# A longer scan in the planner's table, and reciprocal norms spread by a repeated column

## The chip, the cores and the metric

The kernel runs on one core of a Trainium2 chip. The metric is the device time of one launch in microseconds; the kernel before took 1902.8 us, the median of three runs (1902.1 to 1905.98).

## The reference

Two layers of a backbone over 512 latent and 256 context tokens, 1024 channels, float32. Each layer: RMS norm with a modulation, one wide input projection, three mixers beside each other, a gated merge, an output projection and a residual add. A last RMS norm ends it.

```python
def rms_norm(x, g):
    y = xf * lax.rsqrt(jnp.mean(xf * xf, axis=-1, keepdims=True) + EPS)
    return (y * g).astype(x.dtype)

h = rms_norm(x, norm_g) * (1 + scale[:, None]) + shift[:, None]
aq, ..., gm = split_proj(h @ w_in)       # A: differential attention, B: mLSTM, C: neighbourhood attention
b = jnp.cumsum(lfc, axis=1)              # B: running sums of log forget gates, in chunks of 64
m_new = jnp.maximum(bL + m, jnp.max(g_s, axis=-1))   # B: and a running maximum over the chunks
x = x + gate[:, None] * merge_branches((y_a, y_b, y_c), gm, w_br, w_out)
```

The two parts that matter here are the norm, whose 1/rms is one number per token, and the mLSTM gates, whose running sums and maxima are scans over the 768 tokens.

## The kernel before

Activations are held transposed, channels on the partitions and tokens along the free axis, in eight tiles of 128 channels. A product in float32 is made of three matmuls of rounded halves (high by high, high by low, low by high); the low half of a weight tile (`wh<-wr,wh`) is subtracted on POOL or DVE, the high half cast on ACT. Each layer runs the branches C, A, B one after the other, then the merge, then the output projection ("finish"). In every branch the input projection of the next head (`pj<-h,wh`) is the filler of TensorE, and the attention of the heads before it (scores `gp<-qk` or `sc<-qk`, transposes `gp<-ident,p`, products with the values) is put between.

The order on each engine is written by a planner while the program is built. `Timed` (L324) wraps each engine and gives every instruction a price in ns (L341 to L349); `Sched` keeps one clock per engine, and lets a task issue its next TensorE instruction only when the planner's clocks say that its inputs are there. So a price that is too low makes the planner put dependent TensorE work too early; the engines run their lists in order, and on the chip TensorE then waits. The price of a VectorE instruction of n elements per partition is n / 0.96 + 69 ns; `tensor_tensor_scan` has no rule of its own. The lists are fixed at build time: nothing is reordered on the chip.

The three scans of a layer (L1409, L1411, L1418 in `branch_b_gates`) stand in the C branch on VectorE, between its softmax steps. The scores of C go through a ring of three PSUM tiles (`gp`): the fourth pair of scores can start only when ACT has taken the exponential of the first (`p<-gp,m`), and that waits for the row extremes (`m<-gp`) on VectorE. After the scans, twelve transposes `gp<-ident,pt` bring their results into columns, which VectorE copies to `bcol`.

`norm_rows` (L729) makes 1/rms: transposes of the summed squares, a reduction into columns (`ms`), nine small VectorE steps of `rsqrt_cols` that end in `rr` (128 tokens on the partitions, one column per block of tokens). To have it along the free axis on all partitions, it multiplies `ident` by each column into a diagonal matrix in a tile `dg` of the ring `p` (L746), and multiplies `ones` by it on TensorE (L751): row j of the result is r of token j everywhere. It is called once at the start (768 tokens, six blocks), twice at the end of layer 0 (512 and 256 tokens) and twice at the end of layer 1 (256 each).

Of the kernel before, what the change touches and what calls it, by code (L numbers as in the profile page):

```python
# [12 lines left out]
F32 = mybir.dt.float32  # L13
# [4 lines left out]
ALU = mybir.AluOpType  # L18
# [7 lines left out]
T = S + L  # L26
# [80 lines left out]
class Sched:  # L107
# [104 lines left out]
    def acq(self, tag, want=None, n=1):  # L212

        while True:
            now = self.T["P"] + (0.0 if want else self.EARLY)
            if not (want == "P" and self.late()) and sum(t <= now for t in self.free[tag]) >= n:
                break
            yield want
        for _ in range(n):
            self._take(tag, now)  # L220
# [5 lines left out]
    def wait(self, flag, n, want=None):  # L226
        while flag.n < n:
            yield want
        self.cur.t = max(self.cur.settle(), flag.t)
        yield want  # L230

    def hit(self, flag, n=1):
        flag.n += n
        flag.t = max(flag.t, self.stamp())
# [63 lines left out]
def _space(ap):  # L298
    return getattr(ap, "space", None)


def _elems(ap):
    n = 1
    for s in list(ap.shape)[1:]:
        n *= int(s)
    return n


class Timed:
# [5 lines left out]
    def __getattr__(self, name):  # L315
        f = getattr(self.real, name)

        def call(*args, **kw):
            aps = [v for v in list(args) + list(kw.values()) if hasattr(v, "shape")]
            n = max(_elems(v) for v in aps)  # L320
            small = sum(1 for v in aps if _elems(v) == 1 and n > 1)
            psum = any(_space(v) == PSUM for v in aps[1:] + aps[:1])
            writes = [kw["out"] if "out" in kw else args[0]]
            if "accum_out" in kw:  # L324
                writes.append(kw["accum_out"])
            if name == "tensor_tensor_reduce":
                writes.append(args[-1])
            reads = [v for v in aps if not any(v is w for w in writes)]
            if name == "dma_start":
                out = kw["out"]  # L330
                self.sched.dma(int(out.shape[0]), int(out.shape[0]) * _elems(out) * 4, reads, writes)
                return f(*args, **kw)  # L332
            if self.eng == "D":
                one = len([v for v in aps if _elems(v) == n]) <= 2 and name in ("tensor_copy", "tensor_scalar", "memset")
                cost = n / (1.92 if one and not psum else 0.96) + 69.0 + 61.0 * small
                if name == "reciprocal":
                    cost = 69.0 + 8.0 * n
                if name == "tensor_tensor_reduce":
                    cost += 220.0
            elif self.eng == "A":  # L340
                cost = n * 0.8333 + (51.0 if psum else 93.0) + 93.0 * small  # L341
            else:
                cost = n * 2.15 + 130.0
            self.sched.run(self.eng, cost, reads, writes)
            return f(*args, **kw)  # L345
        return call
# [3 lines left out]
def kernel(ctx: ExitStack, tc: tile.TileContext, a: dict, out: bass.AP):  # L350
# [10 lines left out]
    const = ctx.enter_context(tc.tile_pool(name="const", bufs=1))  # L361
# [4 lines left out]
    S_ = Sched(bufs)  # L366
    acq, rel, wait, hit = S_.acq, S_.rel, S_.wait, S_.hit
    V, ACT, GP, SY = (Timed(e, r, S_) for e, r in (("D", nc.vector), ("A", nc.scalar), ("G", nc.gpsimd), ("S", nc.sync)))

    def ring(tag, shape, dt=F32):  # L370
        t = rings[tag].tile([128] + list(shape), dt, tag=tag, name=tag)
        S_.fresh(tag, t)
        return t

    def small(n, name, dt=F32):
        return sm_.tile([128, n], dt, tag=name, name=name)

    def mm(o, l, r, start, stop, cost=None):
        n = _elems(o)
        S_.run("P", cost or (max(107.0, 0.4167 * n) + 2.0 if l.dtype != F32 else 1.67 * max(n, 128)), [l, r], [o])  # L380
        PE.matmul(o, l, r, start=start, stop=stop)  # L381

    def tr(o, i, idn):
        S_.run("P", 109.0, [i, idn], [o])
        PE.transpose(o, i, idn)  # L385
# [36 lines left out]

    ident = const.tile([128, 128], F32, name="ident")
    make_identity(nc, ident)
    ones = const.tile([128, 128], F32, name="ones")
    V.memset(ones, 1.0)

    V.memset(cfz, 0.0)
    cf = cfz[:, :, 0:2]
# [296 lines left out]
            rel("t")  # L726
        hit(aflag)

    def norm_rows(acc, n, dg, aflag, res, nflag, tags):  # L729

        nt = n // 128
        yield from wait(aflag, KD, "P")
        ms, r = small(NT, "ms"), small(NT, "rr")
        for t0 in range(0, nt, 4):
            m = min(4, nt - t0)
            yield from acq("gp", "P")
            p = ring("gp", [512])
            for b in range(m):
                tr(p[:, 128 * b:128 * b + 128], acc[:, 128 * (t0 + b):128 * (t0 + b) + 128], ident)
            yield  # L740
            V.tensor_reduce(ms[:, t0:t0 + m], p[:, :128 * m].rearrange("p (b d) -> p b d", d=128), axis=AX.X, op=ALU.add)
            rel("gp")
        V.tensor_scalar(ms[:, :nt], ms[:, :nt], 1.0 / D, EPS, ALU.mult, ALU.add)
        yield from rsqrt_cols(r[:, :nt], ms[:, :nt], nt, "rt")
        for b in range(nt):
            V.tensor_scalar(dg[:, 128 * b:128 * b + 128], ident, r[:, b:b + 1], None, ALU.mult)  # L746
        for o in range(0, n, 512):
            w = min(512, n - o)
            yield from acq("gp", "P")
            p = ring("gp", [512])  # L750
            mm(p[:, :w], ones, dg[:, o:o + w], True, True)  # L751
            res.append(p[:, :w])
        hit(nflag)
        for t in tags:
            rel(t)
# [35 lines left out]
    def layer(l, x, h, hfl):  # L791
# [942 lines left out]
        def finish(mh, mhf):  # L1734
            S_.need("qk"), S_.need("qk")
            xs, pairs = x_tiles()
            for k in range(KD):
                SY.dma_start(out=xs[k][:, :nq], in_=xin[:, k, :nq] if l == 0 else xdr[k])
            S_.need("p"), S_.need("p")
            acc, dg = ring("p", [T]), ring("p", [T])  # L1740
            fs = [[Flag(), Flag()] for _ in range(KD)]
            for s, (o, n) in enumerate(wsegs(l)):
                kind = 0 if o < S else 1
                aflag, nflag, res = Flag(), Flag(), []
                for d in range(KD):
                    def done(si, ps, o, n, d=d, kind=kind, aflag=aflag):
                        def fin():
                            xd = xs[d][:, o:o + n]
                            yield from wait(modf[l][4 + d // 4], 1)
                            V.scalar_tensor_tensor(xd, ps[:, :n], modc[l][:, 16 + d, kind:kind + 1], xd, ALU.mult, ALU.add)  # L1750
                            rel("pj")
                            yield "S"
                            if not last and kind == 0:
                                SY.dma_start(out=xdr[d], in_=xd)
                                S_.cur.landed = 0.0
                            yield from sumsq(acc[:, o:o + n], xd, aflag, d)
                        S_.urgent(fin())
                    proj(("wout", d, s), [(o, n)], done, mh, ready=lambda k: need(mhf[k][kind]))
                S_.calm(norm_rows(acc[:, o:o + n], n, dg[:, o:o + n], aflag, res, nflag, ("p", "p") if s else ()))
                row = lambda res=res: res[0]  # L1760
                if not last:
                    all_h(l + 1, s, xs, mh, row, nflag, fs)
                    continue

                def give(k, o=o, n=n, row=row, nflag=nflag):
                    yield from wait(nflag, 1)
                    for i in range(k, k + 2):
                        xd = xs[i][:, o:o + n]
                        V.scalar_tensor_tensor(xd, xd, prm[0][:, PRM_FG + i:PRM_FG + i + 1], row(), ALU.mult, ALU.mult)
                        yield None if i == k else "S"  # L1770
                    SY.dma_start(out=out[:, k:k + 2, o:o + n], in_=pairs[k // 2][:, :, o:o + n])
                for k in range(0, KD, 2):
                    S_.calm(give(k))
            return xs, mh, fs
# [4 lines left out]
        return finish(*merge())  # L1779


    S_.need("p"), S_.need("p")
    acc, dg = ring("p", [T]), ring("p", [T])
    aflag, nflag, res = Flag(), Flag(), []
    for k in range(KD):
        S_.calm(sumsq(acc, x0[k], aflag, k))
    S_.calm(norm_rows(acc, T, dg, aflag, res, nflag, ("p", "p")))
    h, hfl = [], [[Flag(), Flag()] for _ in range(KD)]
    for k in range(KD):
        S_.need("h")  # L1790
# [124 lines left out]
```

## Time and profile before

| | |
|---|---|
| median of the runs | 1902.8 us |
| the profiled execution | 1903.77 us, span 1902.0 us |
| TensorE busy | 1813.3 us, 95% of the span |
| VectorE busy | 1343.8 us, 71% |
| ScalarE, GpSimd busy | 858.0 us, 643.1 us |
| mean granted TensorE clock | 0.987 |

The profile describes one execution. PE is TensorE's matmuls, PEld its weight loads, DVE VectorE, ACT ScalarE, POOL GpSimd. Nearly all lines read L345 (the wrapper's call), L381 (matmul) or L385 (transpose), since helpers issue everything; what an instruction does is read from the tiles' names and shapes. In a timeline, a row merges neighbours of a kind (x is their count), and the bracket at its end says how long the engine stood idle before it and which engine's instruction ended that. Scans are shown by the order listing as SCALAR_TENSOR_TENSOR and by the trace as TENSOR_TENSOR_SCAN.

### The profile page before, as it was taken

What the parts mean: (1) busy time and instruction counts of PE and PEld (TensorE: products, weight loads), DVE (VectorE), ACT (ScalarE), POOL (GpSimd) and SP (SyncE); (2) the same over time, 40 slices, a digit from 0 to 9 for tenths busy, and PEclk for the clock granted to TensorE, in tenths of its full rate; (3) what the DMA queues carried; (4) which work ended last, traced back from release to release, by engine and by line L of the source; (5) the groups of instructions that cost most, each with busy time, mean ns of one, the idle gap of its engine ahead of it and who ended that gap; (6) DMA issues with size and microseconds to landing.
All of it is one profiled execution on the core that took longest, in us unless ns stands there. A gap on an engine that the chain in (4) does not pass through costs nothing. (4 is left out here: it accounts for less than half of the span.)

```text
span 1902.0 us, 31909 instructions
## 1 busy us (share of the span) xinstructions
PE 1813.3 (95%) x11140; PEld 1602.3 (84%) x11140; DVE 1343.8 (71%) x3168; ACT 858.0 (45%) x1932; POOL 643.1 (34%) x563
## 2 busy tenths in 40 slices
PE   5999999999999999999999889999999899999996
PEld 2989998988899888888888778898888787888886
DVE  6676767888887875777763887766887788733346
ACT  4455555555555453222233354644555444533343
POOL 1332322221223322333335343423212324344454
PEclk9999999999999999999999899999999999999998
DMA  8333422222342443666546334333222434545453
GB/s 324 91 106 97 116 81 82 64 78 65 104 118 82 118 154 126 220 195 202 193 153 217 112 98 124 108 92 101 76 67 62 145 89 131 158 159 162 160 169 127
DMA packets 148479, 243.56 MB, mean 128 GB/s; under 512 B 18400, under 2 KB 52544, under 8 KB 148320
## 3 DMA queue, kind: packets, MB, share of 16 engines
q1 hardware_dynamic: 148320, 241.53, 40.8%
q8 instruction: 88, 1.44, 0.3%
q14 instruction: 71, 0.58, 0.1%
HBM read 199.45 MB, written 27.33 MB: 119 GB/s over the span
## 5 line engine op out<-in xcount | busy, mean ns | idle before, releaser
L381 PE MATMUL pj<-h,wh 128*128 128x512 f32 (+1 forms) x5664 | 1110.6, 349 | 3.1 <-ACT h L345 1.8
L381 PEld LDWEIGHTS pj<-h,wh 128*128 128x128 f32 x5664 | 895.7, 191 | 122.0 <-ACT h L345 2.4
L345 POOL TENSOR_TENSOR wh<-wr,wh 128x512 fp32r<-128x512 f32 (+1 forms) x409 | 562.3, 1382 | 1114.4 <-ACT wh L345 1066.6
L345 ACT CAST wh<-wr 128x512 fp32r<-128x512 f32 (+1 forms) x416 | 256.4, 621 | 377.9 <-PE pj L381 213.1
L381 PE MATMUL pj<-wh,h 128*128 128x256 f32 (+1 forms) x1728 | 239.4, 290 | 6.3 <-DVE h L345 4.9
L381 PEld LDWEIGHTS pj<-wh,h 128*128 128x128 f32 x1728 | 220.8, 193 | 10.1 <-DVE h L345 7.3
L345 DVE TENSOR_TENSOR pt<-gp,pt 128x512 fp32r<-128x512 f32 (+1 forms) x224 | 123.9, 572 | 87.4 <-ACT pt L345 86.4
L345 ACT CAST pt<-gp 128x512 fp32r<-128x512 f32 (+1 forms) x224 | 105.5, 496 | 151.7 <-PE gp L385 151.1
L381 PE MATMUL pj<-v,wh 128*128 128x512 f32 (+1 forms) x576 | 159.7, 356 | 0.1
L385 PE MATMUL gp<-ident,p 128*128 128x128 f32 x720 | 110.6, 276 | 17.6 <-DVE p L345 11.8
L381 PE MATMUL gp<-pt,v 128*128 128x256 f32 x864 | 117.4, 283 | 0.1
L381 PEld LDWEIGHTS pj<-v,wh 128*128 128x128 f32 x576 | 102.9, 189 | 15.6 <-DVE t L345 0.5
L385 PEld LDWEIGHTS gp<-ident,p 128*128 128x128 f32 x720 | 84.3, 141 | 36.1 <-issue 17.5
L381 PEld LDWEIGHTS gp<-pt,v 128*128 128x128 f32 x864 | 110.8, 191 | 2.3 <-DVE pt L345 0.3
L345 ACT ACTIVATE t<-pj 128x512 f32<-128x512 f32 (+1 forms) x118 | 63.5, 538 | 102.1 <-PE pj L381 100.7
L381 PE MATMUL pj<-qk,wh 128*128 128x512 f32 (+1 forms) x288 | 102.4, 356 | 0.8 <-DVE qk L345 0.7
L345 DVE SCALAR_TENSOR_TENSOR t<-t,pj 128x512 f32<-128x512 f32 x66 | 38.5, 594 | 75.4 <-PE pj L381 75.4
L381 PE MATMUL sc<-qk 128*128 128x512 f32 (+1 forms) x360 | 83.3, 340 | 7.8 <-ACT p L345 4.9
L345 DVE TENSOR_REDUCE mna<-sc 128x1 f32<-128x768 f32 (+1 forms) x80 | 67.7, 846 | 31.1 <-PE sc L381 30.7
L345 ACT ACTIVATE p<-sc,mna 128x768 f32<-128x768 f32 (+1 forms) x80 | 65.6, 820 | 47.4 <-DVE mna L345 47.1
L345 DVE CUSTOM_DVE_ANT_0 sc<-cb,dt 128x512 f32<-128x512 f32 x56 | 58.9, 1052 | 33.0 <-DMA cb<-in_wmodr_dram 31.8
L345 DVE CUSTOM_DVE_ANT_0 sc<-cb,prm 128x512 f32<-128x512 f32 x56 | 61.5, 1099 | 26.1 <-DMA cb<-in_wmodr_dram 24.8
(145 smaller groups left out, 2095.0 us busy)
## 6 DMA issues: line engine op xcount, KB each, us to landing
wr<-in_wu_dram SPq DMA_DIRECT2D x296, 256.0 KB, 2.9
cb<-in_wmodr_dram SPq DMA_DIRECT2D x64, 256.0 KB, 3.7
wr<-in_wout_dram SPq DMA_DIRECT2D x64, 256.0 KB, 2.9
p<-afd SPq DMA_DIRECT2D x80, 192.0 KB, 4.2
wr<-in_wbr_dram SPq DMA_DIRECT2D x48, 256.0 KB, 2.8
q<-qk SPq DMA_DIRECT2D x160, 64.0 KB, 2.2
cb<-vd SPq DMA_DIRECT2D x32, 256.0 KB, 3.3
qk<-in_xT_dram SPq DMA_DIRECT2D x16, 384.0 KB, 6.3
```

Source lines behind the costliest of these rows:

```text
L345: return f(*args, **kw)
L381: PE.matmul(o, l, r, start=start, stop=stop)
L385: PE.transpose(o, i, idn)
```

## The change

A scan of n elements is now priced at n / 0.48 + 430 ns, which for 768 elements is 2030 ns in place of 869 ns. And `norm_rows` no longer makes the diagonal: the column `rr` is repeated 128 times (a stride of zero) as the stationary operand and `ident` is the moving one, one matmul of 128 columns for each block. The tiles `dg` and `ones` go. Both change what the planner's clocks say, so the order changes downstream as well.

```diff
@@ Timed.call
                 if name == "tensor_tensor_reduce":
                     cost += 220.0
+                if name == "tensor_tensor_scan":
+                    cost = n / 0.48 + 430.0
...
-    ones = const.tile([128, 128], F32, name="ones")
-    V.memset(ones, 1.0)
...
-    def norm_rows(acc, n, dg, aflag, res, nflag, tags):
+    def norm_rows(acc, n, aflag, res, nflag, tags):
...
         yield from rsqrt_cols(r[:, :nt], ms[:, :nt], nt, "rt")
-        for b in range(nt):
-            V.tensor_scalar(dg[:, 128 * b:128 * b + 128], ident, r[:, b:b + 1], None, ALU.mult)
         for o in range(0, n, 512):
             w = min(512, n - o)
             yield from acq("gp", "P")
             p = ring("gp", [512])
-            mm(p[:, :w], ones, dg[:, o:o + w], True, True)
+            for b in range(o // 128, (o + w) // 128):
+                mm(p[:, 128 * b - o:128 * b - o + 128], r[:, b:b + 1].to_broadcast([128, 128]), ident, True, True)
             res.append(p[:, :w])
...
@@ finish, and the start likewise
-            S_.need("p"), S_.need("p")
-            acc, dg = ring("p", [T]), ring("p", [T])
+            S_.need("p")
+            acc = ring("p", [T])
```

In the listings the line numbers shift: L345, L381 and L385 of before are L347, L383 and L387 now.

First place: TensorE in the C branch of layer 0, from the third to the fourth pair of scores of the branch (`gp<-qk` and `gp<-qk,q`, two matmuls each), with projection work between. Before:

```order
L381 MATMUL gp<-qk,q_858 128x256 x2
L381 MATMUL pj<-h,wh 128x512 x3
L381 MATMUL pj<-h,wh 128x256 x6
L381 MATMUL gp<-qk 128x256 x2
L381 MATMUL gp<-qk,q_858 128x256 x2
L381 MATMUL pj<-h,wh 128x256 x18
```

And now:

```order
L383 MATMUL gp<-qk,q_852 128x256 x2
L383 MATMUL pj<-h,wh 128x512 x3
L383 MATMUL pj<-h,wh 128x256 x18
L383 MATMUL gp<-qk 128x256 x2
L383 MATMUL gp<-qk,q_852 128x256 x2
L383 MATMUL pj<-h,wh 128x256 x6
```

Twelve projection matmuls of 256 columns have moved ahead of the fourth pair.

Second place: the same pairs of scores on TensorE in the C branch of layer 1. Before:

```order
L381 MATMUL gp<-qk,q_12732 128x256 x2
L381 MATMUL pj<-h,wh 128x256 x6
L381 MATMUL pj<-h,wh 128x512 x3
L381 MATMUL gp<-qk 128x256 x2
L381 MATMUL gp<-qk,q_12732 128x256 x2
L381 MATMUL pj<-h,wh 128x512 x18
L385 MATMUL gp<-ident,pt 128x112 x2
```

And now:

```order
L383 MATMUL gp<-qk,q_12724 128x256 x2
L383 MATMUL pj<-h,wh 128x256 x6
L383 MATMUL pj<-h,wh 128x512 x21
L383 MATMUL gp<-qk 128x256 x2
L383 MATMUL gp<-qk,q_12724 128x256 x2
L383 MATMUL pj<-h,wh 128x512 x6
```

Eighteen projection matmuls of 512 columns have moved ahead of the fourth pair, and the transposes `gp<-ident,pt` stand 33 projection matmuls behind that pair in place of 18.

The same place on VectorE, from the third scan (`v<-v,pt 112x768`) to the row extremes `m` that release the fourth pair. Before:

```order
L345 SCALAR_TENSOR_TENSOR v<-v,pt 112x768
L345 TENSOR_TENSOR v<-pt,v 112x768
L345 COPY pt<-v 48x768
L345 TENSOR_REDUCE m_12802<-gp 128x1
L345 ISA p,m_12805<-gp,cb,m_12802 128x256
```

And now:

```order
L347 SCALAR_TENSOR_TENSOR v<-v,pt 112x768
L347 TENSOR_REDUCE m_12792<-gp 128x1
L347 ISA p,m_12795<-gp,cb,m_12792 128x256
L347 ISA m_12795 128x1
L347 TENSOR_REDUCE m_12809<-gp 128x1
L347 ISA p,m_12812<-gp,cb,m_12809 128x256
L347 TENSOR_TENSOR v<-pt,v 112x768
```

The extremes now stand right behind the scan, ahead of the add and the copy. In layer 0 the same two rows have moved behind them.

Third place: TensorE at the end of layer 0, from the transposes of the first norm to its spread (`gp<-p,ones` before, `gp<-ident,rr` now). Before:

```order
L385 MATMUL gp<-ident,p 128x128 x4
L381 MATMUL pj<-h,wh 128x256 x54
L381 MATMUL gp<-p,ones 128x512
L381 MATMUL pj<-h,wh 128x256 x102
L381 MATMUL pj<-wh,h 128x272 x36
```

And now:

```order
L387 MATMUL gp<-ident,p 128x128 x4
L383 MATMUL pj<-h,wh 128x256 x42
L383 MATMUL gp<-ident,rr 128x128 x4
L383 MATMUL pj<-h,wh 128x256 x114
L383 MATMUL pj<-wh,h 128x272 x36
```

The spread stands twelve projection matmuls earlier. The other three norms' spreads stand: at the start one matmul earlier, ahead of the columns of the modulation (`gp<-csel,t`); in the second norm of layer 0 where they stood; in the first norm of layer 1 six matmuls earlier; at the very end where it stood.

In layer 0 the order of attention work against projection work differs in branch C and early in branch A, and is the same again from there to the layer's end; in layer 1 it differs from the scans to the end of branch B. Of the low halves of the weights, two move from VectorE to POOL (six and 402 of 128x512 before, four and 404 now).

## Rows read from the trace of the kernel before

**Rows 1.** Page: span, and busy time by engine

```profile
span 1902.0 us, 31909 instructions
...
PE 1813.3 (95%) x11140; PEld 1602.3 (84%) x11140; DVE 1343.8 (71%) x3168; ACT 858.0 (45%) x1932; POOL 643.1 (34%) x563
```

**Rows 2.** Timeline of PE: start, us, what, [idle before <-releaser]

```profile
100.15 0.80 PE L381 MATMUL gp<-qk 128*128 128x256 f32 x2 [3.02 <-ACT p L345]
...
1042.39 6.71 PE L381 MATMUL pj<-h,wh 128*128 128x256 f32 x54
...
1052.25 2.08 PE L381 MATMUL gp<-p,ones 128*128 128x512 f32 x2 [3.15 <-DVE p L345]
...
1105.31 16.62 PE L381 MATMUL pj<-h,wh 128*128 128x512 f32 x72
...
1134.27 0.80 PE L381 MATMUL gp<-qk 128*128 128x256 f32 x2 [6.94 <-ACT p L345]
...
1893.81 1.19 PE L381 MATMUL gp<-p,ones 128*128 128x256 f32 x2 [3.50 <-DVE p L345]
```

**Rows 3.** Waits of PE: who for whom, us in total, times, longest

```profile
PE gp L381 <- ACT p L345: 10.7, 3, 6.9
...
PE gp L385 <- DVE bcol L345: 1.9, 2, 1.3
```

**Rows 4.** Windows: stretch, length, busy PE PEld DVE ACT POOL, then PEclk, DMA, GB/s

```profile
100.00:104.00 4.00, 3.85 (x21) 3.85 (x22) 3.61 (x14) 2.84 (x9) 0.57 (x1) 0.61 0.31 74
...
1052.20:1056.00 3.80, 3.75 (x14) 2.71 (x15) 2.45 (x5) 0.77 (x2) 0.00 (x0) 0.58 0.24 86
...
1134.00:1138.00 4.00, 3.73 (x12) 3.20 (x13) 3.75 (x12) 3.16 (x8) 1.28 (x1) 0.58 0.47 130
```

**Rows 5.** Windows in layer 1, branches A and B

```profile
1370.00:1390.00 20.00, 16.71 (x78) 13.29 (x77) 15.91 (x38) 8.28 (x20) 2.95 (x2) 0.83 0.19 53
1390.00:1662.00 272.00, 258.85 (x1547) 224.55 (x1545) 218.96 (x549) 137.81 (x310) 86.66 (x86) 1.00 0.39 113
```

**Rows 6.** Lines of DVE: group xcount | busy, mean ns | idle before

```profile
L345 DVE TENSOR_TENSOR_SCAN pt<-pt,t 112x768 f32<-112x768 f32 x4 | 7.5, 1904 | 0.1
...
L345 DVE TENSOR_SCALAR p<-ident,rr 128x128 f32<-128x128 f32 x16 | 5.5, 401 | 0.1
```

**Rows 7.** Timeline of ACT: the exponential behind the layer-1 extremes

```profile
1133.66 0.47 ACT L345 ACTIVATE p<-gp,m 128x256 f32<-128x256 f32 x1 [8.23 <-DVE m L345]
```

**Rows 8.** Timeline of DVE around the third scan, layer 0 then layer 1

```profile
96.26 1.23 DVE L345 TENSOR_TENSOR v<-pt,v 112x768 f32<-112x768 f32 x1
97.50 0.90 DVE L345 COPY pt<-v 48x768 f32<-48x768 f32 x1
98.43 0.42 DVE L345 TENSOR_REDUCE m<-gp 128x1 f32<-128x256 f32 x1
...
1127.20 1.91 DVE L345 TENSOR_TENSOR v<-v,pt 112x767 f32<-112x767 f32 x1
1129.15 1.82 DVE L345 TENSOR_TENSOR_SCAN v<-v,pt 112x768 f32<-112x768 f32 x1
1131.00 0.96 DVE L345 TENSOR_TENSOR v<-pt,v 112x768 f32<-112x768 f32 x1
1131.97 0.56 DVE L345 COPY pt<-v 48x768 f32<-48x768 f32 x1
1132.56 0.42 DVE L345 TENSOR_REDUCE m<-gp 128x1 f32<-128x256 f32 x1
```

**Rows 9.** Timeline of DVE at the diagonals: end of layer 0, end of layer 1

```profile
1049.40 2.79 DVE L345 TENSOR_SCALAR p<-ident,rr 128x128 f32<-128x128 f32 x4
...
1893.18 0.48 DVE L345 TENSOR_SCALAR p<-ident,rr 128x128 f32<-128x128 f32 x2
```

**Rows 10.** Timeline of PEld at the last spread

```profile
1893.78 0.50 PEld L381 LDWEIGHTS gp<-p,ones 128*128 128x128 f32 x2 [3.71 <-issue]
```

**Rows 11.** Timeline of POOL beside the scans of layer 1

```profile
1126.31 1.98 POOL L345 TENSOR_TENSOR wh<-wr,wh 128x512 fp32r<-128x512 f32 x1
```

More of the change, by code (lines that the diff above doesn't have):

```diff
@@ L1758, in finish @@
                     proj(("wout", d, s), [(o, n)], done, mh, ready=lambda k: need(mhf[k][kind]))
-                S_.calm(norm_rows(acc[:, o:o + n], n, dg[:, o:o + n], aflag, res, nflag, ("p", "p") if s else ()))
+                S_.calm(norm_rows(acc[:, o:o + n], n, aflag, res, nflag, ("p",) if s else ()))
                 row = lambda res=res: res[0]
@@ L1779, in layer @@
         return finish(*merge())
-    S_.need("p"), S_.need("p")
-    acc, dg = ring("p", [T]), ring("p", [T])
+    S_.need("p")
+    acc = ring("p", [T])
     aflag, nflag, res = Flag(), Flag(), []
@@ L1786 @@
         S_.calm(sumsq(acc, x0[k], aflag, k))
-    S_.calm(norm_rows(acc, T, dg, aflag, res, nflag, ("p", "p")))
+    S_.calm(norm_rows(acc, T, aflag, res, nflag, ("p",)))
     h, hfl = [], [[Flag(), Flag()] for _ in range(KD)]
```

## The prediction

> **What bounds the kernel now.** I read the page first, then TensorE's waits, then its timeline for the idle pieces, then windows behind the long ones, and last VectorE and POOL at those places. TensorE is busy for 1813.3 of 1902.0 us [rows 1], so the span is its work plus 88.7 us in which it stands. The matmul work is nearly the same after the change, so I ask only which of those idle microseconds go, and which come. The reader is to see that the waits are few and long in three places: at the fourth pair of scores in branch C, once in each layer (3.02 and 6.94 us), and at the first spread at the end of layer 0 (3.15 us); 3.50 us at the last spread lies on the way to the end [rows 2]. The two score waits are nearly all of a single row among the waits, PE for ACT's exponential; the columns of the scan results cost 1.9 us more [rows 3].
>
> A long wait costs twice. Behind each of the three the granted clock is 0.61, 0.58 and 0.58 of full speed over about 4 us, a mix of the 1.2 and the 2.4 GHz level [rows 4], so work that would go at full speed loses 4.0 x 0.39 = 1.6, 3.8 x 0.42 = 1.6 and 4.0 x 0.42 = 1.7 us. Waits short enough leave the clock: from 1390 to 1662 us TensorE stands for 272 - 258.9 = 13.1 us in all, and the clock reads 1.00 [rows 5].
>
> **Part one: the price of the scan.** The chip takes 1.9 us for a scan [rows 6], the planner charged 0.87 us and now charges 2.03 us. No scan gets faster; what pays is that TensorE's list stops asking for results the chip does not have. Why TensorE stood: ACT's exponential waited 8.23 us for the row extremes [rows 7], which stood behind the scans on VectorE, and there behind an add and a copy that nobody on TensorE needs soon [rows 8].
>
> Layer 0. The fourth pair is reached 12 matmuls of 256 columns later; one takes 6.71 / 54 = 0.124 us [rows 2], so 1.5 us. The extremes no longer wait for the add and the copy, 1.23 + 0.90 = 2.1 us [rows 8]. Together 3.6 us against a wait of 3.02 us: it goes, and with it the slow clock. 3.0 + 1.6 = 4.6 us.
>
> Layer 1. The pair is reached 18 matmuls of 512 columns later, 18 x 16.62 / 72 = 4.2 us [rows 2], and the extremes come 1132.56 - 1131.00 = 1.6 us earlier [rows 8]. Left of 6.94 us: 1.2 us, too little to pull the clock, by the short waits of [rows 5]. Gain 5.8 + 1.7 = 7.5 us. The wait for the columns (1.9 us) goes as well, since the transposes now have 33 projection matmuls ahead of them behind that pair, not 18: 9.4 us for layer 1. The lower bound here is that only the moved order counts and the clock falls again: 4.2 us.
>
> The work passed over is not lost: the projection matmuls that move ahead are TensorE's own, done in the time it stood. On VectorE the add and the copies come later, and what waits for them are the columns, whose transposes are later too. Two weight halves move to POOL, on an engine that is busy for 643 of 1902 us [rows 1]; I cost them at nothing, and at 4.0 us if TensorE should come to wait for both, at the 1.98 us of one [rows 11].
>
> **Part two: the spread.** Sixteen VectorE instructions of 0.401 us go [rows 6], 6.4 us of an engine that is off the path at most times. What counts is where each norm ends.
>
> End of layer 0. The reciprocals were ready when the four diagonals began, at 1049.40; the diagonals ended 2.79 us later [rows 9], and the spread began at 1052.25 after 3.15 us of idle time [rows 2], so TensorE arrived at 1049.1. Now it arrives 12 x 0.124 = 1.5 us earlier, at 1047.6, and starts at about 1049.5, with those 1.5 us of work still to do: 1052.25 - 1049.5 - 1.5 = 1.3 us gained. It stands for 1.9 us rather than 3.15, so I take the clock as kept: 1.3 + 1.6 = 2.9 us, with 1.3 us if it falls. VectorE, which makes the next layer's `h` behind it, starts 2.8 us earlier too, so I see nothing that takes this back.
>
> The last norm. Two diagonals, 0.48 us [rows 9], go from the path to the end. Against it: two weight loads become four, at 0.25 us each [rows 10], hidden or not; 0 to 0.5 us, I take 0.3. The start, the second norm of layer 0 and the first of layer 1: the spread is ready earlier by the diagonals that stood before it, and TensorE has about as much more work behind it as it waits less. I take 0; at the start the bounds are the six diagonals, 6 x 0.401 = 2.4 us of gain, and a loss of 1.0 us for eight more weight loads at 0.25 us of which half show.
>
> The loads are where the Trainium skill speaks against the change: "TensorE: Matmul & The Clock Gate", section Weight-path perf modes, says that the fast weight load is not used for float32. By that rule all the new loads stay slow, as the float32 loads of `ones` were; the trace agrees in that those took 0.25 us each [rows 10]. If none were hidden the last norm would give 0.0 in place of 0.3.
>
> **The sum.** 4.6 + 9.4 + 2.9 + 0.3 = 17.2 us. Against it stands what the new order costs in the stretches it shuffles: I take 3 us, one wait as long as that of layer 0's scores, because work that TensorE now reaches sooner is made by engines that did not get faster. 17.2 - 3 = 14.2 us off 1903.8 us (the profiled execution) is 1889.6; that execution is 1.0 us above the median of the runs, 1902.8, which becomes 1888.6. I say 1889 us.
>
> **The rivals.** *The layer-1 stall stays in part.* For: VectorE is late there for a reason that the planner still has no price for. The subtraction ahead of the third scan took 1.91 us where the add of that shape behind it took 0.96 us [rows 8], and POOL's weight half lay beside it from 1126.31 to 1128.29 [rows 11]. If three such instructions stretch by about 0.95 us each, the extremes come 2.9 us later, the wait left is 4.1 us and the clock falls again: 2.9 + 1.7 = 4.6 us less, 1894 us. The Trainium skill has a rule for it, in "SBUF — State Buffer", section SBUF: two separate sides: VectorE and GpSimd share a port pair under an exclusive lock, and the loser waits for the winner's whole instruction. The trace agrees in that one row pair; by the rule the stretch depends on where POOL's work falls, which shifts with the order. Against: the 18 matmuls alone cover 4.2 us.
>
> *It is given back.* TensorE reaches the branches A and B of layer 1 some 9 us ahead of where it was, while VectorE is busy there for 219 of 272 us [rows 5]. If the 13.1 us of idle time there become 28 us, about 2 us of the 17.2 remain: 1901 us. For: that stretch has the densest waits left. Against: an engine at 80% can catch up, and the planner again places work where its clocks allow.
>
> *Slower.* The shuffle makes new stalls with a fall of the clock in branches A and B. One cluster of that kind stands there now, from 1370 to 1390 us: 3.3 us idle and a clock of 0.83, together 3.3 + 20 x 0.17 = 6.7 us [rows 5]. Three more of these cost 20.1 us and outweigh 17.2; with four the time is 1903 + 26.8 - 17.2 = 1912 us. It decides from the third. For: the order differs from the scans of layer 1 to the end of its branch B. Against: 2.5 of them would be needed merely to break even, and there is one in the whole of layer 1's attention.
>
> **How the numbers follow.** Forecast 0.57, the stall in part 0.14, given back 0.16, slower 0.11, and 0.02 for a shuffle that also removes the cluster at 1370. Runs of this kernel tell about 0.2%, 3.8 us, from no change. Faster: 0.57 + 0.14 + 0.02 = 0.73; the same 0.16; slower 0.11. The low end is the full sum with one lucky 6.7 us cluster gone, 1902.8 - 17.2 - 6.7 = 1879; the high end takes in most of the second rival, 1902. That leaves out less than 2 in 10.
>
> **What would show it.** Right: TensorE's waits for ACT's exponential at `gp<-qk` fall from 10.7 us to under 2 us, the clock reads 1.00 behind the scans of both layers, the columns' wait is gone, the first spread of layer 0 waits for `rr` under 2 us, TensorE's busy time falls by some 5 us (less slow clock) and its idle time by 8 to 12 us. Wrong: the windows behind the fourth pair still read 0.6; or they read 1.00, and the idle time from the scans of layer 1 to the end of its branch B has grown by more than 10 us.

## The result, and the profile after

The changed kernel takes 1893.8 us, the median of five runs (1891.98 to 1895.11), beside 1902.8 us for the kernel before on the same chip (1900.84 to 1905.98): a ratio of 0.9946, 95% interval 0.9932 to 0.996. It is faster by 9 us, about 0.5%. The forecast was 1889 us, 1879 to 1902 in range. The profiled execution took 1891.98 us.

The page of the changed kernel, to be read against [rows 1]: TensorE's busy time fell by 3.9 us, and what it stood fell from 88.7 to 1890.2 - 1809.4 = 80.8 us.

```profile
span 1890.2 us, 31916 instructions
...
PE 1809.4 (96%) x11160; PEld 1606.1 (85%) x11160; DVE 1324.6 (70%) x3149; ACT 859.5 (45%) x1932; POOL 647.1 (34%) x565
```

TensorE's waits in it (who for whom, us in total, times, longest), to be read against [rows 3]:

```profile
PE gp L387 <- DVE p L347: 12.0, 16, 2.2
PE gp L383 <- DVE rr L347: 8.7, 4, 3.0
PE gp L387 <- DVE pt L347: 8.6, 2, 6.7
...
PE gp L383 <- ACT p L347: 3.8, 3, 1.6
```

The wait for ACT's exponential fell from 10.7 to 3.8 us; the forecast was under 2. And a row that was not among the long ones, the transposes' wait for VectorE's `pt`, now has 8.6 us. TensorE's timeline shows where, and answers to [rows 2]: the first row stands at layer 0's fourth pair of scores (3.02 us before), the second at the transposes of the scan results behind it, the third at the spread that ends layer 0 (3.15 before), then layer 1's third and fourth pairs (6.94 before at the fourth), the new wait, and the last spread (3.50 before).

```profile
109.45 0.50 PE L383 MATMUL gp<-qk 128*128 128x256 f32 x2 [0.84 <-ACT p L347]
...
118.17 0.60 PE L387 MATMUL gp<-ident,pt 112*128 112x112 f32 x4 [1.94 <-DVE pt L347]
...
1045.97 1.16 PE L383 MATMUL gp<-ident,rr 128*128 128x128 f32 x8 [1.76 <-DVE rr L347]
...
1126.40 0.50 PE L383 MATMUL gp<-qk 128*128 128x256 f32 x2 [1.42 <-ACT p L347]
...
1131.25 0.51 PE L383 MATMUL gp<-qk 128*128 128x256 f32 x2 [1.56 <-ACT p L347]
...
1131.82 4.27 PE L383 MATMUL pj<-h,wh 128*128 128x512 f32 x18
1135.94 0.60 PE L387 MATMUL gp<-ident,p 128*128 128x128 f32 x4
1143.19 1.11 PE L387 MATMUL gp<-ident,p 128*128 128x128 f32 x4 [6.65 <-DVE pt L347]
...
1881.99 1.20 PE L383 MATMUL gp<-ident,rr 128*128 128x128 f32 x4 [2.98 <-DVE rr L347]
```

So layer 1's stall did not go: it ends 12 us behind the start of the fourth pair, at the transposes of the softmax rows and no longer at the scores, and nearly kept its length. The windows that answer to [rows 4] say the same of the clock: 1.00 behind the fourth pair of layer 0 and at the norm (0.61 and 0.58 before), 0.76 around the new wait. In the branches behind, the clock reads 1.00 from 1370 to 1390 us (0.83 in [rows 5]), and over the 272 us behind that TensorE stands for 7.8 us, not 13.1.

```profile
105.00:125.00 20.00, 16.93 (x105) 14.20 (x103) 18.76 (x54) 10.04 (x25) 5.40 (x6) 1.00 0.40 114
1045.00:1060.00 15.00, 14.03 (x117) 14.03 (x118) 12.92 (x20) 10.12 (x20) 10.75 (x8) 1.00 0.49 143
1138.00:1152.00 14.00, 8.81 (x60) 8.81 (x61) 10.84 (x38) 3.06 (x10) 1.81 (x3) 0.76 0.23 72
1370.00:1390.00 20.00, 18.54 (x112) 15.96 (x111) 18.72 (x42) 10.23 (x25) 5.01 (x4) 1.00 0.32 87
1390.00:1662.00 272.00, 264.21 (x1566) 229.63 (x1564) 219.10 (x580) 141.44 (x319) 88.08 (x89) 0.99 0.39 115
```

The cluster of stalls that stood at 1370 us is not simply gone, though. One of its kind stands some 30 us earlier in the changed kernel, and before has none there; TensorE's timeline and the window behind it:

```profile
1338.92 0.85 PE L387 MATMUL gp<-ident,p 128*128 128x128 f32 x6 [2.25 <-DVE p L347]
1341.39 0.72 PE L383 MATMUL sc<-qk 128*128 128x512 f32 x2 [1.62 <-ACT p L347]
```

```profile
1340.00:1350.00 10.00, 8.61 (x34) 7.07 (x35) 6.48 (x20) 3.32 (x8) 0.00 (x0) 0.83 0.01 2
```

What VectorE does from the second scan to the `pt` that ends the wait (its timeline in the changed kernel, cut to the rows that matter; in the whole list no gap of over 0.2 us stands between two rows):

```profile
1117.41 2.03 DVE L347 TENSOR_TENSOR_SCAN pt<-pt,t 112x768 f32<-112x768 f32 x1
1119.47 1.22 DVE L347 TENSOR_TENSOR v<-pt 112x768 f32<-112x768 f32 x1
1120.73 1.94 DVE L347 TENSOR_TENSOR v<-v,pt 112x767 f32<-112x767 f32 x1
1122.70 2.09 DVE L347 TENSOR_TENSOR_SCAN v<-v,pt 112x768 f32<-112x768 f32 x1
1124.71 0.39 DVE L347 TENSOR_REDUCE m<-gp 128x1 f32<-128x256 f32 x1
...
1126.63 1.89 DVE L347 TENSOR_TENSOR v<-pt,v 112x768 f32<-112x768 f32 x1
...
1131.60 0.56 DVE L347 COPY pt<-v 48x768 f32<-48x768 f32 x1
...
1134.85 1.96 DVE L347 COPY pt<-v 48x768 f32<-48x768 f32 x2
...
1137.56 1.25 DVE L347 TENSOR_SCALAR p<-p,smc 128x512 f32<-128x512 f32 x1
...
1141.37 1.16 DVE L347 COPY pt<-v 64x512 f32<-64x512 f32 x4
1142.46 0.68 DVE L347 TENSOR_TENSOR pt<-gp,pt 128x512 fp32r<-128x512 f32 x1
```

From 1117.41 to 1142.46 us are 25.05 us of VectorE; the planner's clock gave the same rows 20.9 us. TensorE's list was built for a VectorE 4.1 us further on.

Since the order differs, equal times in two kernels are not equal work. The ledger below gives each matmul the time that its form usually takes from one start to the next (the 40th percentile over all runs; the spreads' own matmuls count as nothing), and compares the moments at which TensorE has done the same sum. Entries are microseconds gained (-) or lost (+) against before in that stretch, whose ends are times of before: C of layer 0 is 80 to 135, the rest of layer 0 to 1030, its last norm to 1100, C of layer 1 to 1160, the rest to 1840. A row adds up to the difference of the two profiled spans. They come from one execution each; two with one list differ by up to 3 at the start and about 2 in another stretch. The profiled run of before is 1.0 us above its median, that of the changed kernel 1.8 us below, so the first row adds up to 11.8 us where the medians give 9.0; that of the planner with POOL's overlap is 5.5 us above, that of the price alone 2.6 us.

| kernel | start | C, layer 0 | rest | norm | C, layer 1 | rest | end |
|---|---|---|---|---|---|---|---|
| changed | +2.1 | -0.3 | -5.2 | -2.9 | +0.2 | -5.7 | 0.0 |
| price alone | +3.0 | -0.2 | -5.3 | +0.3 | +0.8 | -3.8 | +0.4 |
| spread alone | +1.5 | +0.2 | -2.0 | -1.6 | +1.4 | -0.4 | -0.7 |
| VectorE charged 4.1 us | +1.5 | -4.4 | +7.8 | -1.5 | +0.7 | -2.5 | -0.2 |
| planner with POOL's overlap | +3.9 | -0.5 | +10.3 | +1.4 | +6.0 | -9.9 | -2.2 |
| price 2250 | +1.3 | -2.3 | +3.1 | -2.8 | -0.3 | -1.0 | -0.3 |
| price in layer 1 only | +0.8 | +1.1 | -2.0 | -2.6 | +0.4 | -4.9 | -0.3 |
| changed, copies on ACT | +0.6 | -2.7 | -4.9 | -2.6 | -3.2 | -4.7 | -0.3 |
| changed, POOL empty there | +1.1 | +0.7 | -5.6 | -1.6 | -7.2 | -3.7 | -0.5 |
| before, copies on ACT | 0.0 | -0.9 | -1.6 | -1.3 | -3.6 | -0.3 | +0.5 |
| copies on ACT, new plan | +2.8 | -2.6 | +7.9 | -2.9 | -5.6 | -12.0 | -0.7 |

The first row tells the result: the two C branches, where the price was meant to act, are worth nothing, the norm's entry is what was forecast, and the rest comes from branches that have no scan in them. Two entries say less than they seem to. Of the 5.2 us in the rest of layer 0 about 2 belong to the one execution of before: the three runs with its order there (the spread alone, the price in layer 1 only, before with copies on ACT) have 1.6 to 2.0 as well. And at the norm a kernel that keeps the diagonals (before with copies on ACT) has 1.3. In layer 1, by the same reckoning in finer steps, the cluster at 1370 us gives about 5 us and the new one at 1338 us takes about 5; what is left of the gain arises behind 1420 us.

### The profile page after: what moved, and what is told of

Read it like the earlier page. It is cut to its first block, busy times and chain, and to the rows that moved or that the text cites. A ratio compares the mean times of both kernels' runs of the same rounds, so it can differ in the third digit from the quotient of the medians.

```text
span 1890.2 us, 31916 instructions
## 1 busy us (share of the span) xinstructions
PE 1809.4 (96%) x11160; PEld 1606.1 (85%) x11160; DVE 1324.6 (70%) x3149; ACT 859.5 (45%) x1932; POOL 647.1 (34%) x565
## 4 chain that ended last, share of the span: by engine, by line
PE 71%; DVE 14%; issue 6%; POOL 5%; ACT 3%; DMA 1%; SPq 0%; POOLq 0%; DVEq 0%; ACTq 0%
PE pj L383 54%; PE gp L383 8%; PE gp L387 5%; POOL wh L347 4%; PE sc L383 4%; DVE p L347 3%; DVE qk L347 3%; DVE pt L347 1%; DVE t L347 1%; ACT p L347 1%; DVE h L347 1%; DVE hs L347 1%; DMA pt<-in_wmod_dram 0%; ACT wh L347 0%; DVE gz L347 0%
## 5 line engine op out<-in xcount | busy, mean ns | idle before, releaser
L383 PE MATMUL pj<-h,wh 128*128 128x512 f32 (+1 forms) x5664 | 1108.4, 349 | 3.1 <-ACT h L347 1.8
L383 PEld LDWEIGHTS pj<-h,wh 128*128 128x128 f32 x5664 | 895.1, 190 | 120.8 <-ACT h L347 2.3
L347 POOL TENSOR_TENSOR wh<-wr,wh 128x512 fp32r<-128x512 f32 (+1 forms) x411 | 567.0, 1387 | 1090.8 <-ACT wh L347 1038.5
L347 ACT CAST wh<-wr 128x512 fp32r<-128x512 f32 (+1 forms) x416 | 256.8, 621 | 388.9 <-PE pj L383 225.7
L383 PE MATMUL pj<-wh,h 128*128 128x256 f32 (+1 forms) x1728 | 244.0, 293 | 6.5 <-DVE h L347 3.6
L383 PEld LDWEIGHTS pj<-wh,h 128*128 128x128 f32 x1728 | 224.9, 197 | 10.6 <-DVE h L347 6.1
L347 DVE TENSOR_TENSOR pt<-gp,pt 128x512 fp32r<-128x512 f32 (+1 forms) x224 | 124.3, 572 | 82.5 <-ACT pt L347 81.2
L347 ACT CAST pt<-gp 128x512 fp32r<-128x512 f32 (+1 forms) x224 | 106.3, 495 | 136.9 <-PE gp L387 135.9
L383 PE MATMUL pj<-v,wh 128*128 128x512 f32 (+1 forms) x576 | 159.7, 356 | 0.0
L387 PE MATMUL gp<-ident,p 128*128 128x128 f32 x720 | 112.1, 276 | 20.8 <-DVE p L347 12.0
L387 PEld LDWEIGHTS gp<-ident,p 128*128 128x128 f32 x720 | 84.3, 141 | 39.0 <-issue 12.3
L383 PE MATMUL gp<-pt,v 128*128 128x256 f32 x864 | 117.0, 283 | 0.0
L383 PEld LDWEIGHTS pj<-v,wh 128*128 128x128 f32 x576 | 102.9, 189 | 15.1
L383 PEld LDWEIGHTS gp<-pt,v 128*128 128x128 f32 x864 | 110.9, 191 | 2.1
L347 ACT ACTIVATE t<-pj 128x512 f32<-128x512 f32 (+1 forms) x118 | 63.3, 536 | 104.3 <-PE pj L383 104.3
L383 PE MATMUL pj<-qk,wh 128*128 128x512 f32 (+1 forms) x288 | 102.2, 355 | 0.0
L347 DVE SCALAR_TENSOR_TENSOR t<-t,pj 128x512 f32<-128x512 f32 x66 | 38.5, 593 | 85.1 <-PE pj L383 85.1
L347 DVE TENSOR_REDUCE mna<-sc 128x1 f32<-128x768 f32 (+1 forms) x80 | 67.7, 847 | 40.3 <-PE sc L383 39.9
L383 PE MATMUL sc<-qk 128*128 128x512 f32 (+1 forms) x360 | 82.3, 337 | 7.2 <-ACT p L347 6.6
L347 ACT ACTIVATE p<-sc,mna 128x768 f32<-128x768 f32 (+1 forms) x80 | 65.6, 820 | 46.4 <-DVE mna L347 46.0
L347 DVE CUSTOM_DVE_ANT_0 sc<-cb,prm 128x512 f32<-128x512 f32 x56 | 62.9, 1123 | 27.3 <-DMA cb<-in_wmodr_dram 26.0
L347 DVE CUSTOM_DVE_ANT_0 sc<-cb,dt 128x512 f32<-128x512 f32 x56 | 58.2, 1039 | 31.1 <-DMA cb<-in_wmodr_dram 30.0
```

## The experiments

The theory: in a C branch with scans VectorE sets the pace, so a later list on TensorE only moves the place where it stands; the gain is the norm's, and that of the particular order in which the later branches come out. The rivals were the prediction's account and, for the long VectorE rows, a cause other than POOL.

### The two parts apart

```diff
+                if name == "tensor_tensor_scan":
+                    cost = n / 0.48 + 430.0
```

The scan's price alone. Expected: 

> The kernel before with the new price of the scan alone; the diagonals and the matmul by ones stay. Its order is that of the changed kernel but for the spread. Theory (the two profiles laid beside each other, step by step of TensorE's list): in both C branches what the moved scores win is given back a few us later at the transposes, so C is worth nothing, and what the price brings comes from the branches A and B of layer 1, some 6 to 9 us: 1894 to 1897 us, with TensorE's wait of about 6.6 us for VectorE's pt at gp<-ident,p in layer 1 still there, and the wait of 3.15 us at the first spread of layer 0 as before or about 1.5 us longer. Rival (the account of the prediction): the price is worth 11 to 14 us, 1889 to 1892 us. Second rival: the price brings nothing by itself, and the gain is the spread's: 1901 to 1904 us.

Measured: 1896.4 us, ratio 0.9964 (0.9951 to 0.9976). And the other part alone, the changed kernel without those two lines: 

> The changed kernel without the new price: the order is that of before but for the spread. Theory: 2.9 us at the norm at the end of layer 0 and 0.5 us at the last one, against 1.5 us at the start, where the clock comes up later, and 1.5 us at the first norm of the last layer, where a wait of 2 us lets the clock fall: 1901 to 1903 us, the same as before within what can be told. The account of the prediction: 3.2 us gained, 1899.5 us. If the gain is mostly the spread's: below 1897 us.

Measured: 1902.2 us, ratio 0.9996 (0.9985 to 1.0007). Both times are as the theory had them, and the prediction's 11 to 14 us for the price are ruled out. In the ledger the price alone gains in neither C branch, and TensorE's wait of 6.65 us for `pt` is there. Its gain does not stand where the theory had put it, though: 3.8 us in the branches of layer 1 and not 6 to 9, and 5.3 in those of layer 0. The spread alone has 1.6 us at the norm and little else that can be told from no change.

### Correct the rest of the plan

If TensorE's list asks too early because VectorE is 4.1 us late, charge it:

```diff
+                S_.run("D", 4100.0, [], [xf[64:R]])
                 V.tensor_copy(xf[64:R], aa[64:R, ::-1])
```

> The changed kernel, and the planner's VectorE clock charged with 4.1 us more in each layer ahead of the first copy pt<-v of the scan results (no instruction is added): that is how much later than its plan VectorE was there in layer 1 of the changed kernel. Theory A (the price of these rows is what is still missing): TensorE reaches the transposes later, its wait of 6.65 us for pt in layer 1 falls under 2 us and the clock there reads 1.00; 5 to 9 us faster than the changed kernel, 1885 to 1889 us. Theory B (VectorE is the bound of this stretch, busy without a gap from 1109 to 1147 us, and a later list only shifts where TensorE stands): idle time and slow clock from 1100 to 1160 us add up to within 2 us of what they are now, and the time lies at 1891 to 1897 us.

Measured: 1905.7 us, ratio 1.0011 (1.0002 to 1.0021), slower than both theories allowed, and 12 us slower than the changed kernel. In C of layer 0 the charge did what theory A wanted (4.4 us gained); the rest of that layer then lost 7.8. In layer 1 TensorE stood again, now for the exponentials ahead of the transposes. TensorE's timeline of this kernel:

```profile
1149.55 1.11 PE L387 MATMUL gp<-ident,p 128*128 128x128 f32 x4 [6.30 <-ACT p L347]
1152.97 1.12 PE L387 MATMUL gp<-ident,p 128*128 128x128 f32 x4 [2.32 <-ACT p L347]
```

So under three lists a stall of 6.3 to 6.9 us stands in that branch, each time for another result, and C of layer 1 costs the same (+0.7): theory B for that stretch, while its time for the whole kernel was wrong, since the branches behind were drawn anew.

A planner that stretches VectorE's rows by the POOL work beside them, everywhere:

```diff
...
+            for a, b in self.pool:
+                if a < end:
+                    end += b - max(a, start)
...
```

> The changed kernel with a planner that lets a VectorE instruction with two large inputs in SBUF, or a single one at twice the rate, last longer by the time in which a POOL instruction lies beside it in the plan; nothing else is changed, but the whole order shifts. In the trace of the changed kernel such rows last longer by about that overlap (v<-pt,v 112x768: 0.96 us alone, 1.89 us with a POOL row beside it), and rows that read PSUM do not. Theory A: with VectorE's clock nearer to the chip the waits on VectorE (pt, p, rr) shrink in both layers, 1880 to 1888 us, and the wait of 6.65 us is gone. Theory B (the order is shuffled, VectorE is no faster): 1889 to 1898 us, some waits go and others come.

Measured: 1907.2 us, ratio 1.0024 (1.0012 to 1.0036). Both theories missed. The ledger runs from +10.3 to -9.9 by stretches. So this price list made no better order. How much truer it is stays open: it also charges VectorE for POOL rows that begin after VectorE's own, and in the trace these cost VectorE nothing (last section).

### Is it the order behind?

```diff
...
-                if name == "tensor_tensor_scan":
+                if name == "tensor_tensor_scan" and self.sched.layer == 1:
...
```

> The changed kernel with the new price of the scan in layer 1 alone; the order of layer 0 is then that of before but for the spread, and VectorE's list of layer 1 is nearly that of the changed kernel. Theory (what the price brings arises in the branches A and B of layer 1, from the order that its C branch hands on): 1894 to 1898 us, with layer 1 as fast as in the changed kernel, and layer 0 as with the spread alone. Rival (the gain needs the price in layer 0): 1900 to 1904 us.

Measured: 1894.7 us, ratio 0.9958 (0.9945 to 0.997). As expected: with layer 0's order that of the spread alone, the rest of layer 1 still gains 4.9 us.

```diff
-                    cost = n / 0.48 + 430.0
+                    cost = n / 0.48 + 650.0
```

> The changed kernel with the scan priced at 2250 ns in place of 2030; the scans of the changed kernel took 2.1 us in six rows of mean length, so this price is about as near to the chip. Theory A (what the price brings is the price's: TensorE asks later for what the scans make): within 3 us of the changed kernel, 1890 to 1896 us. Theory B (what it brings is the particular order of the branches behind it): anywhere from 1890 to 1908 us, with the order of all branches behind the first scan different, and a difference of over 4 us from the changed kernel as likely as not.

Measured: 1901.5 us, ratio 0.9993 (0.9981 to 1.0005). The six scans of the changed kernel last 2.20 us on average, so this price is no worse than 2.03, and the gain is gone, as theory B allowed. This kernel does lose C's stalls in layer 0 (-2.3); it loses 3.1 in the rest of layer 0, and the rest of layer 1 gives 1.0 in place of 5.7.

### What VectorE's time is worth with TensorE's list kept

Here only the engine of an instruction is changed. The planner is charged for the old one, so TensorE's list stays word for word, and the ledger's other stretches move by 2 us at most. First the seven copies of the scan results of each layer, from VectorE to ACT:

```diff
+    VA = Timed("D", Other("tensor_copy", lambda out, in_: nc.scalar.copy(out=out, in_=in_)), S_)
...
-                V.tensor_copy(xf[64:R], aa[64:R, ::-1])
+                VA.tensor_copy(xf[64:R], aa[64:R, ::-1])
```

> The changed kernel with the copies of the scan results (pt<-v, seven in a layer) on ACT; the planner is charged as if they stood on VectorE, so TensorE's and POOL's lists are those of the changed kernel, word for word. Theory (VectorE is the bound behind the scans, whatever TensorE's list asks for): the three groups of copies that stand ahead of VectorE's pt in layer 1 took 0.56 + 1.96 + 1.16 = 3.7 us; TensorE's wait of 6.65 us for pt falls to about 3 us, that of 1.94 us in layer 0 to under 1 us, and the clock behind the long one keeps its level: 1886 to 1890 us. Rival (another chain ends that wait, such as ACT's exponentials, which now stand behind the copies): waits of the same sum elsewhere between 1100 and 1160 us, 1891 to 1896 us.

Measured: 1885.2 us, ratio 0.9914 (0.9898 to 0.993), faster than both kernels. TensorE's timeline, at the row that waited 6.65 us:

```profile
1136.71 0.65 PE L393 MATMUL gp<-ident,p 128*128 128x128 f32 x4 [3.20 <-DVE pt L347]
```

and the window behind it, where the clock reads 0.90 and not 0.76:

```profile
1138.00:1152.00 14.00, 14.00 (x111) 14.00 (x110) 7.83 (x40) 2.89 (x9) 1.28 (x2) 0.90 0.37 101
```

3.45 us of 3.7 expected came off the wait, and the 1.94 us in layer 0 are gone (its fourth pair now waits 1.16 us, where 0.84 stood). VectorE's row that ends TensorE's wait now waits itself for ACT's cast, which stands behind the copies: the relief is used up there.

```profile
1135.97 0.69 DVE L347 TENSOR_TENSOR pt<-gp,pt 128x512 fp32r<-128x512 f32 x1 [0.68 <-ACT pt L347]
```

Then twelve weight halves and eight bias tiles of C of layer 1, taken from POOL. In their place ACT copies one of the two inputs, so this kernel leaves those 20 subtractions out; it only serves to time the rest:

```diff
...
-            (V if far else GP).tensor_tensor(w[:, 1], src, w[:, 0].bitcast(F32), ALU.subtract)
+            (V if far else pick("w", 213, 224, GA)).tensor_tensor(w[:, 1], src, w[:, 0].bitcast(F32), ALU.subtract)
...
```

> The changed kernel, the same lists on TensorE and VectorE, with 12 weight halves and 8 bias tiles of the C branch of layer 1 taken from POOL: in their place ACT copies one input, which leaves out those subtractions. Theory (VectorE's rows there last longer for as long as a POOL row lies beside them): from the second scan to pt six rows have 1.0, 0.3, 0.9, 0.8, 0.3 and 0.8 us more than the same forms elsewhere, 4.1 us together; with POOL empty v<-pt,v takes 0.96 us and not 1.89, p<-p,smc 0.49 and not 1.25, pt starts about 4 us earlier, TensorE's wait of 6.65 us falls to 2 to 3 us: 1887 to 1890 us. Rival (those rows are long for another reason, such as the scan's own reads or the DMAs beside them): durations and wait as they were, 1891 to 1896 us.

Measured: 1886.3 us, ratio 0.9913 (0.9899 to 0.9926). VectorE's timeline in this kernel, the same rows as of the changed kernel above:

```profile
1115.95 1.75 DVE L347 TENSOR_TENSOR_SCAN pt<-pt,t 112x768 f32<-112x768 f32 x1
1117.74 0.96 DVE L347 TENSOR_TENSOR v<-pt 112x768 f32<-112x768 f32 x1
1118.73 0.96 DVE L347 TENSOR_TENSOR v<-v,pt 112x767 f32<-112x767 f32 x1
1119.73 1.82 DVE L347 TENSOR_TENSOR_SCAN v<-v,pt 112x768 f32<-112x768 f32 x1
1121.46 0.40 DVE L347 TENSOR_REDUCE m<-gp 128x1 f32<-128x256 f32 x1
...
1123.39 0.95 DVE L347 TENSOR_TENSOR v<-pt,v 112x768 f32<-112x768 f32 x1
...
1130.45 1.03 DVE L347 COPY pt<-v 48x768 f32<-48x768 f32 x2
...
1131.91 0.49 DVE L347 TENSOR_SCALAR p<-p,smc 128x512 f32<-128x512 f32 x1
...
1136.19 0.69 DVE L347 TENSOR_TENSOR pt<-gp,pt 128x512 fp32r<-128x512 f32 x1 [0.19 <-ACT pt L347]
```

Each row that was long is short: 1.94 became 0.96, 1.89 became 0.95, 1.25 became 0.49, and rows that read PSUM (`m<-gp`) are as they were. From the second scan to `pt` are 20.24 us, not 25.05, and TensorE's wait there fell to

```profile
1136.94 0.66 PE L400 MATMUL gp<-ident,p 128*128 128x128 f32 x4 [2.95 <-DVE pt L347]
```

So the time by which VectorE was late is POOL's, shown by taking POOL away: 4.8 us, more than the 4.1 of the plan, since the two scans got shorter too. C of layer 1 alone gains 7.2 us against before; in layer 0, where POOL keeps its work, the wait at the transposes of the scan results stays (1.93 us).

### The relief in the old order, and with a new plan

The same seven copies on ACT in the kernel before, TensorE's list kept: 

> The kernel before with the copies of the scan results on ACT, charged as if they stood on VectorE: TensorE's list is that of before, word for word. Theory (in the order of before the long waits stand at the fourth pair of scores, ahead of which in VectorE's list only one 0.90 us copy stands, in layer 0; the other copies come behind): the 3.02 us in layer 0 fall to about 2.1, the 6.94 us in layer 1 stay, the columns' waits may go: 1 to 4 us, 1898 to 1901 us. So the new price is what made this relief worth 6 to 9 us. Rival (the relief is worth the same in either order): 1892 to 1896 us.

Measured: 1897.1 us, ratio 0.9973 (0.9961 to 0.9984), 5.6 us and between the two expectations. The wait at the fourth pair of layer 1 fell only to 6.20 us, as expected, but the columns' waits went and C gained 3.6. The claim that the price made the relief worth more is not borne out in C of layer 1: the copies' move gains 3.4 us there in the changed order and 3.6 in the old one. In C of layer 0 it gains 2.4 and 0.9, in the whole kernel 0.32% and 0.27% by the ratios; that difference is within the two intervals.

And with the planner told that the copies run on ACT, the order planned anew: 

> The changed kernel with the same copies on ACT, and the planner told so: it charges ACT for them, and the order is planned anew, different from layer 0's C branch on. Theory (the relief of VectorE in the C branches is some 6 us as with the order kept, and what the branches behind it do with a fresh order is a draw of plus or minus 8 us): anywhere from 1880 to 1900 us, with the stalls for pt at the scans of both layers under 3 us together. Rival (a planner that knows where the copies run does better with them): 1880 to 1886 us.

Measured: 1890.7 us, ratio 0.9938 (0.9924 to 0.9952), 5.5 us slower than the same relief with the order kept (4.6 us when each is held against its own runs of before). A planner that knows where the copies run did no better with them. C gains 2.6 and 5.6 us in the two layers, its `pt` waits are down to 0.3 us; the rest of layer 0 lost 7.9 and the rest of layer 1 gained 12.0.

## Why the prediction was right, and where it was not

The direction and the range held; the time is 4.8 us above the forecast, and a gain of 14.2 us lies outside the interval. The mechanism of the largest term did not hold. Of the signs that were named, the waits for the exponential (3.8 us, not under 2) and the clock behind layer 1's scans (1.00 behind the scores, 0.76 behind the new wait) went against it; the columns' wait (0.2 us), the wait for `rr` (1.76) and the idle time (7.9 us less) came out as said or nearly so. Step by step:

- *Layer 0's scores, 4.6 us.* The wait went (0.84 us left) and the clock stayed at 1.00: some 4 us were in hand at 105 us by the ledger's clock. By 135 us they were gone, 1.94 of them to the transposes of the scan results (the four 64x512 copies ahead of them took 3.17 us, beside POOL rows, where four such took 1.16 in layer 1). Net gain 0.3. The step that failed, here and in layer 1, is "the work passed over is not lost": it costed VectorE's later add and copies at nothing, because what waits for them is later too. It was not later enough.
- *Layer 1's scores and columns, 9.4 us.* This term failed. The extremes did come in time (1.42 and 1.56 us left, of 6.94), and behind the scores TensorE led by some 15 us, 8.6 of them won there. Then it stood 6.65 us for `pt`, with the clock at 0.76. Net loss 0.2. I asked what waits for the rows that the extremes overtook, and named only the columns; queued behind the same rows stood the low halves `pt<-gp,pt` that free the transposes' tile. VectorE was busy without a gap there, so what was moved ahead on it made something else late.
- *POOL.* The rival of a stall that stays in part named the cause, POOL's rows beside VectorE's, and 1894 us. That time came out by chance, with the gains of the later branches in it; the place did not: it had the extremes late, and late was what stands 18 us behind the first of them on VectorE (1142.46 against 1124.71). The Trainium skill, "SBUF — State Buffer", section SBUF: two separate sides, has the exclusive lock that I weighed and set aside; the runs agree with it (1.89 us became 0.95 with POOL empty).
- *The norm, 2.9 us.* The wait is 1.76 us (expected 1.9), the clock 1.00, and the ledger has 2.9. The part that comes from the shorter wait holds; that the clock kept its level, 1.6 of the 2.9, was partly luck. With POOL empty in layer 1 the same wait is 1.75 us, and the clock reads 0.89 from 1045 to 1060 us; in before with copies on ACT the diagonals' wait is 3.15 us as ever, and the clock reads 1.00 there. Eight of the nine kernels with the spread have 1.5 to 2.9 us at the norm.
- *The last norm, 0.3 us.* Right in size: 2.98 us of wait against 3.50, and from its transposes to the end of the span 11.6 us against 12.1. *The start, 0.* The changed kernel's first 80 us took 2.1 us more, the same list with copies on ACT 0.6, and the price alone, whose list there is that of before, 3.0; no loss that can be told from the scatter.
- *Give-back, 3 us.* The sign was wrong. The stretches behind the scans gained 5.2 and 5.7 us, about 2 of the first being the one execution of before. But the four plans that price the scan in both layers and differ from the changed kernel in more than the spread all lost in that of layer 0, 3.1 to 10.3 us. It is the order drawn, not a benefit of a truer price: price 2250 has the same reason and no gain. I found no single wait that carries these gains; the 13.1 and 7.8 us of standing in branches A and B are spread over many waits, of at most 2.6 us. Why this plan and not another stays open.

So the sum came near by luck, by two errors of opposite sign: of 14.0 us for the stalls at the scans 0.1 is left, and orders that I had booked as a loss of 3 us gained 10.9 by the ledger.

## What to carry to other kernels

When a list is reordered so that an engine no longer waits, look at the engine it waited for: if that one is busy without a gap, expect the wait to turn up at the next thing queued there; here only work taken off it paid. To measure such relief, keep every other list as it is (charge the planner for the old engine); here that gave 1885.2 us, and the same edit with a new plan 1890.7. A planner's price, even a truer one, redraws everything behind it, and here one timing of it said little about the price.

## What the runs showed of the hardware

Of the VectorE rows shown above, those with all operands in SBUF last longer when a POOL row is already running as they begin (`v<-v,pt` 1.94 us, 0.96 with POOL empty; `p<-p,smc` 1.25 and 0.49), and those that read a PSUM tile do not (`m<-gp` 0.39 and 0.40). For the rows named here the extra time is what is left of that POOL row, less 0.1 to 0.2 us. `v<-v,pt` begins at 1120.73 and takes 0.98 us more; the first POOL row below ends at 1121.85, 1.12 us later. A VectorE row that begins first keeps its time, and then POOL's row is the longer one: `qk<-t,qk` takes 0.95 us as with POOL empty, and the POOL row that begins 0.06 us behind it 2.02 us, where half of its form take 1.3 or less.

```profile
1119.84 2.01 POOL L347 TENSOR_TENSOR wh<-wr,wh 128x512 fp32r<-128x512 f32 x1
...
1128.61 2.02 POOL L347 TENSOR_TENSOR wh<-wr,wh 128x512 fp32r<-128x512 f32 x1 [0.90 <-ACT wh L347]
```

```profile
1128.55 0.95 DVE L347 TENSOR_TENSOR qk<-t,qk 64x768 fp32r<-64x768 f32 x1
```

The scans are no exception. The third scan of layer 1 stretched little (2.09 and 1.82 us) because little of POOL's row was left (0.5 us); that of layer 0 began with 1.12 us left and took 2.73 us. I had weighed this as a matter of single rows; in a stretch where VectorE is full it was 4.8 of 25 us.
